# Ordering a whole encoder layer's instructions with another model of the machine

## The chip, the cores and the metric

The kernel runs on one core of a Trainium2 chip. The metric is the device time of one execution, in microseconds (us). The engines are TensorE (PE; its weight loads are listed as PEld), VectorE (DVE), ScalarE (ACT), GpSimd (POOL) and SyncE (SP, which here only issues DMAs).

## The reference

One encoder layer is applied to two sequences, `x_prompt` (1024 tokens) and `x_sample` (512 tokens), each of width 1024, in float32:

```
h  = x + token_mixer(rmsnorm(x))
h  = h + square(relu(rmsnorm(h) @ w_up)) @ w_down        # width 4096
y  = rmsnorm(h)

token_mixer(xn):
    z = xn @ w_in            # q_A k_A v_A q_B k_B v_B gate_A gate_B
    o_A = attention of 8 heads over all tokens, 2 key/value heads,
          q and k normalised and rotated
    o_B = attention of 8 heads over a clamped 8 x 16 window of the token grid,
          with a learned bias by relative position
    return (sigmoid(gate_A) * (o_A @ w_proj_a)
            + sigmoid(gate_B) * (o_B @ w_proj_b)) @ w_out
```

## The kernel before, in words

**Numbers.** Every float32 product is made of three matmuls: each operand is cut into a high part (an ACT copy into the matmul's format) and a low part (a DVE subtraction of that copy), and `mm3` (L194 to L197) adds high x high, high x low and low x high in PSUM. So each operand that TensorE takes has passed ACT and DVE before (`split`, L184 and L190; `cut`, L1273 and L1274).

**Stages.** The sequence of 512 tokens is worked through first, then that of 1024, each in this order (`run`): normalisation, and per group `g` of four heads the projections of branch A (`z`, `zv`), then the sweep of branch A (`s_tile`, L740 to L749: scores, row maximum, exponential, reciprocal, scaling on GpSimd; then transposes at L783, the cut into high and low at L788 and L789, and the product with V, `pv`, L759 and L760). Then branch B (`s_unit`, L971 to L982; `t_unit`, L994 to L1000; `v_unit`, L1013), its projections `qkproj` in between, and the merge (`ppa`, `ppb`, `op`). After both sequences comes the MLP over all 1536 tokens in two blocks of 768, with seven products of half-size blocks in place of eight (`up`, its products `ua` to `ud`; and the down projection, `dn`, whose stages run over 26 pairs of product and column group, six steps each). There the left operands are loaded as `ar` three pairs of steps ahead (`a_dma`) and cut two steps ahead (`a_step`).

**What sets the order.** The kernel's text is a trace: every instruction is written down once, in the order in which the Python code meets it. Matmuls that depend on nothing urgent, the gates (`gate`, tiles `gps`) and the first projection after attention (`proj_a`, tiles `ppa`), are generators in a list `fill`; the attention loops draw a few steps from it (`fill.pull`) between their own, so that TensorE has work while the softmax chain is on the other engines. When the context `tile.TileContext` closes, its scheduler plays the traced program on a model of the machine: on each engine it takes, of the instructions whose inputs are ready in the model, the one that was traced first. The order that comes out is compiled in; each engine then executes its own instructions in that order. Where `tc.keep_in_program_order` is called, the instruction is tied behind the one traced before it on its engine; this is done for most of the first operations of ACT, DVE and SP, and for the last ones of ACT and DVE. By default the model is the library's plain core simulator. Tiles come from pools with a fixed number of buffers (4 banks of PSUM in `pmm`, two double banks in `pbig`), so an instruction that opens a new tile is not ready until a buffer is free.

The whole layer is traced by `encoder(tc, ...)`, which `kernel` calls (L1795) inside the only context. The entry of that context is recorded under L1780, where the program object is made, and its exit (waits for all DMAs, drains, two synchronisations of all engines) under L1795.

Of the kernel before, what the change touches and what calls it, by code (L numbers as in the profile page):

```python
# [57 lines left out]
            self.pull(64)  # L58


@with_exitstack
def encoder(ctx: ExitStack, tc: tile.TileContext, xs, outs, w):
    nc = tc.nc
    dram = ctx.enter_context(tc.tile_pool(name="dram", bufs=1, space=bass.MemoryType.DRAM))
    cst = ctx.enter_context(tc.tile_pool(name="cst", bufs=1))
# [1733 lines left out]
```

## Time and profile before

| | |
|---|---|
| median of 3 runs | 2144.46 us (2144.26 to 2144.7) |
| the profiled execution's own time | 2144.47 us |
| its span, first to last instruction | 2142.7 us |
| mean granted TensorE clock | 0.999 |
| DMA moved | 354.08 MB, 165 GB/s over the span |

The profile tells, for each engine, when an instruction ran and what released it. Busy time is the union of an engine's instructions; matmuls overlap in the records, because the next one begins before the end of the one ahead is recorded. `x228` is a count, `L740` a line of the kernel, and `a<-b,c` what an instruction writes and reads, with buffer numbers left out. In rows by stretch, the first column is the stretch in us from the span's start, the second its length; then come busy times by engine, the granted clock, the busy share of the DMA engines and GB/s. In rows of groups, the numbers behind the bar are busy time in us, the mean of one in ns, and the idle time of the engine just before these instructions with what ended it.

### The profile page before, as it was taken

The page shows a single profiled execution, that of the slowest core. Times are in us where ns is not written, and L with a number is a line of the kernel's source. Part 1 is how long each engine was busy: PE and PEld are TensorE (multiplying, and loading weights), DVE is VectorE, ACT ScalarE, POOL GpSimd, SP SyncE. Part 2 cuts the span into 40 slices and gives each one's busy share as a digit, 9 for nine tenths or more (in the row PEclk, how much of TensorE's full clock was granted, in tenths as well). Part 3 has the DMA queues.
Part 4 walks back from the last instruction along what each step waited for, and adds up shares of the span by engine and source line. Part 5 has one row for each costly group of instructions (what it writes and reads, how often), then busy time and mean ns, then how long its engine had stood idle before and what let it go on. Part 6 is the DMA issues. An engine that isn't in the chain of part 4 may idle for free.

```text
span 2142.7 us, 32089 instructions
## 1 busy us (share of the span) xinstructions
PE 2115.4 (99%) x10967; PEld 1846.9 (86%) x10967; DVE 1462.8 (68%) x2793; ACT 1145.3 (53%) x2511; POOL 356.1 (17%) x446
## 2 busy tenths in 40 slices
PE   9999999999999999999999999999999999999998
PEld 8888778888897888887888899999999988888887
DVE  6665786767657755556882877778777777759563
ACT  6664653767566644555530566566555643434352
POOL 2232310323232223333200200003000000000000
PEclk9999999999999999999999999999999999999999
DMA  6437557520122133433472665578545799688561
GB/s 191 133 99 208 157 162 249 186 71 25 56 78 69 42 95 108 132 117 111 142 234 105 212 198 182 174 243 208 161 145 155 256 353 342 213 275 280 174 201 64
DMA packets 321259, 354.08 MB, mean 165 GB/s; under 512 B 31551, under 2 KB 255431, under 8 KB 321095
## 3 DMA queue, kind: packets, MB, share of 16 engines
q1 hardware_dynamic: 278647, 280.96, 42.0%
q10 hardware_dynamic: 35296, 50.88, 6.8%
q0 software_dynamic: 7152, 20.19, 3.5%
q8 instruction: 87, 1.43, 0.3%
q14 instruction: 77, 0.63, 0.1%
HBM read 264.85 MB, written 87.88 MB: 165 GB/s over the span
## 4 chain that ended last, share of the span: by engine, by line
PE 68%; issue 1%; DVE 1%; DMA 0%; ACT 0%; SPq 0%; POOL 0%; POOLq 0%; ACTq 0%; DVEq 0%
PE dn L196 7%; PE dn L197 7%; PE dn L195 7%; PE ua L195 2%; PE ua L197 2%; PE ua L196 2%; PE ud L195 2%; PE ud L197 2%; PE ud L196 2%; PE uc L195 2%; PE uc L197 2%; PE uc L196 2%; PE gpss L195 2%; PE gpss L197 2%; PE gpss L196 2%; PE ops L197 1%
## 5 line engine op out<-in xcount | busy, mean ns | idle before, releaser
L197 PE MATMUL dn<-wd,al 128*128 128x512 f32 x624 | 242.8, 389 | 0.0
L196 PE MATMUL dn<-wd,ah 128*128 128x512 f32 x624 | 242.8, 389 | 0.0
L195 PE MATMUL dn<-wd,ah 128*128 128x512 f32 x624 | 242.7, 389 | 0.0
L1273 ACT ACTIVATE ah<-ar 128x512 fp32r<-128x512 f32 x168 | 104.2, 627 | 202.6 <-PE dn L196 190.4
L1274 DVE TENSOR_TENSOR al<-ar,ah 128x512 fp32r<-128x512 f32 x168 | 114.0, 686 | 75.3 <-ACT ah L1273 67.2
L195 PEld LDWEIGHTS dn<-wd,ah 128*128 128x128 f32 x624 | 117.2, 188 | 24.5
L197 PEld LDWEIGHTS dn<-wd,al 128*128 128x128 f32 x624 | 117.2, 188 | 24.2
L196 PEld LDWEIGHTS dn<-wd,ah 128*128 128x128 f32 x624 | 117.2, 188 | 24.2
L749 POOL TENSOR_SCALAR ps<-ps,rls 128x1024 f32<-128x1024 f32 (+1 forms) x96 | 96.8, 1009 | 225.7 <-DVE rls L748 200.3
L788 ACT ACTIVATE pths<-pTs 128x512 fp32r<-128x512 f32 x160 | 94.0, 597 | 74.0 <-PE pTs L783 71.8
L789 DVE TENSOR_TENSOR ptls<-pTs,pths 128x512 fp32r<-128x512 f32 x160 | 107.5, 686 | 37.7 <-ACT pths L788 36.7
L743 DVE TENSOR_REDUCE nms<-ss 128x1 f32<-128x1024 f32 (+1 forms) x96 | 99.8, 1040 | 25.6 <-PE ss L741 25.1
L195 PE MATMUL gpss<-xs_0h,w_gs 128*128 128x512 f32 x256 | 105.6, 412 | 0.5 <-DVE ot_Bs L440 0.4
L746 ACT ACTIVATE ps<-ss,nms 128x1024 f32<-128x1024 f32 (+1 forms) x96 | 93.1, 971 | 22.8 <-DVE nms L743 20.1
L783 PEld LDWEIGHTS pTs<-ident,ps 128*128 128x128 f32 x640 | 78.0, 140 | 28.5 <-POOL ps L749 4.3
L180 POOL TENSOR_TENSOR rs_f<-ms_f,mhalf 128x1 f32<-128x1 f32 x6 | 4.0, 667 | 590.7 <-DVE ms_f L176 590.7
L197 PE MATMUL gpss<-xs_0h,w_gs 128*128 128x512 f32 x256 | 101.1, 395 | 0.3 <-DVE w_gs L190 0.3
L196 PE MATMUL gpss<-xs_0l,w_gs 128*128 128x512 f32 x256 | 101.0, 394 | 0.0
L783 PE MATMUL pTs<-ident,ps 128*128 128x128 f32 x640 | 99.0, 274 | 1.3 <-DVE ptls L789 0.6
L1273 ACT ACTIVATE A<-S 128x512 fp32r<-128x512 f32 x128 | 75.9, 623 | 31.2 <-DVE S L1336 22.4
L957 POOL TENSOR_TENSOR bms<-rects,msks 128x384 f32<-128x384 f32 (+1 forms) x72 | 70.1, 976 | 128.7 <-DVE nmbs L974 107.8
L1392 ACT ACTIVATE c<-c 128x384 f32<-128x384 f32 x96 | 50.3, 524 | 69.6 <-DVE c L1391 69.5
(330 smaller groups left out, 6418.7 us busy)
## 6 DMA issues: line engine op xcount, KB each, us to landing
ar<-ud SPq DMA_DIRECT2D x120, 512.0 KB, 5.2
br<-in_w_mlp_down_dram SPq DMA_DIRECT2D x72, 512.0 KB, 5.4
rawu<-in_w_mlp_up_dram SPq DMA_DIRECT2D x64, 512.0 KB, 4.1
ud<-c ACTq DMA_DIRECT2D x128, 192.0 KB, 3.3
raw_gs<-in_w_in_dram SPq DMA_DIRECT2D x32, 512.0 KB, 4.0
zgs<-sgs ACTq DMA_DIRECT2D x48, 256.0 KB, 2.2
ud<-cs SPq DMA_DIRECT2D x64, 192.0 KB
raw_os<-in_w_out_dram SPq DMA_DIRECT2D x16, 512.0 KB, 3.8
```

Source lines behind the costliest of these rows:

```text
L195: nc.tensor.matmul(out, ah, bh, start=start, stop=False, **kw)
L196: nc.tensor.matmul(out, ah, bl, start=False, stop=False, **kw)
L197: nc.tensor.matmul(out, al, bh, start=False, stop=stop, **kw)
L743: nc.vector.tensor_reduce(nm_, s, axis=AX.X, op=ALU.max, negate=True)
L746: nc.scalar.activation(p, s, AF.Exp, bias=nm_, accum_out=l)
L749: nc.gpsimd.tensor_scalar(p, p, rl, 1.0, op0=ALU.mult, op1=ALU.mult)
L783: nc.tensor.transpose(pt[:, j * P : (j + 1) * P], PP[u, j][:, kc * P : (kc + 1) * P], ident)
L788: nc.scalar.activation(hi, pt, AF.Copy)
L789: nc.vector.tensor_tensor(lo, pt, hi.bitcast(F32), op=ALU.subtract)
L957: nc.gpsimd.tensor_tensor(bm.rearrange("p (r c) -> p r c", c=32), rects[h][:, ir : ir + kr_n, jr : jr + 32], msk[:, hf * 3 + ct, :].rearra ...
L1273: nc.scalar.activation(hi, src, AF.Copy)
L1274: nc.vector.tensor_tensor(lo, src, hi.bitcast(F32), op=ALU.subtract)
```

## The change

`encoder` becomes a wrapper; the function that was `encoder` is called `layers` and is not edited. The wrapper opens a critical section of the outer context, and in it a second context on the same program object, with `schedule_with_timeline_sim=True`. That flag makes the scheduler play the program on the library's timeline simulator, a different model of the machine, in place of the plain core simulator. The outer context, which now holds nothing but this section, is still opened and closed by `kernel`. All pins, pools, buffer counts, queues and the text's order stay as they are.

```diff
+def encoder(outer, xs, outs, w):
+    with outer.tile_critical(), tile.TileContext(outer.nc, schedule_with_timeline_sim=True) as tc:
+        layers(tc, xs, outs, w)
+
+
 @with_exitstack
-def encoder(ctx: ExitStack, tc: tile.TileContext, xs, outs, w):
+def layers(ctx: ExitStack, tc: tile.TileContext, xs, outs, w):
     nc = tc.nc
```

## The prediction

> **What bounds the kernel now.** I read the head of the page first, then the busy time of each engine by stage, then the waits of TensorE alone, and last the groups of instructions from which the terms below are made.
>
> ```profile
> span 2142.7 us, 32089 instructions
> ...
> PE 2115.4 (99%) x10967; PEld 1846.9 (86%) x10967; DVE 1462.8 (68%) x2793; ACT 1145.3 (53%) x2511; POOL 356.1 (17%) x446
> ```
>
> TensorE is busy for 2115.4 of 2142.7 us. An order of the instructions changes neither their number nor their work, so all that a new order can win from waiting is 2142.7 - 2115.4 = 27.3 us, 1.3% of the span. The next view says where these 27.3 us lie. Its columns are the stretch, its length, and the busy time of PE, PEld, DVE, ACT and POOL in it.
>
> ```profile
> 0.00:50.00 50.00, 45.10 (x296) 41.80 (x297) 32.44 (x70) 33.62 (x110) 13.45 (x23) 1.00 0.63 184
> 50.00:450.00 400.00, 390.94 (x2085) 330.63 (x2084) 276.18 (x671) 236.55 (x644) 104.56 (x149) 1.00 0.54 167
> 450.00:755.00 305.00, 302.62 (x1700) 256.65 (x1699) 208.81 (x361) 196.78 (x455) 90.09 (x86) 1.00 0.18 55
> 755.00:1030.00 275.00, 273.42 (x1334) 224.95 (x1333) 162.80 (x435) 142.73 (x293) 91.16 (x113) 1.00 0.41 116
> 1030.00:1205.00 175.00, 175.00 (x815) 144.78 (x814) 110.93 (x206) 60.41 (x108) 23.96 (x32) 1.00 0.52 173
> 1205.00:1710.00 505.00, 503.44 (x2873) 496.45 (x2872) 383.00 (x647) 306.83 (x607) 25.61 (x31) 1.00 0.61 190
> 1710.00:2135.00 425.00, 424.94 (x1876) 351.69 (x1874) 286.42 (x407) 166.36 (x292) 6.74 (x11) 1.00 0.73 240
> ```
>
> Subtract the second number from the first in each row. The first 50 us lose 4.9. The two token mixers (50 to 1205 us: projections, the two attentions, gates, merge) lose 9.06 + 2.38 + 1.58 + 0.00 = 13.0. The MLP, from 1205 to 2135 us, loses 1.56 + 0.06 = 1.6, and the last 7.7 us of the span hold no matmul. So an order can win at most 1.6 us in the MLP, nearly half of the program, and what there is to win lies in the mixers and the head.
>
> ```profile
> PE ss L740 <- ACT kTs L594: 2.5, 3, 1.2
> ```
>
> This is the largest entry among TensorE's own waits: 2.5 us in three waits, the longest 1.2. The loss is thus made of many waits of about a microsecond or less at changes from one kind of work to another, and not of one stage with a bottleneck.
>
> **The change, part by part.** It puts the whole program into a second context inside the first and lets another model of the machine choose the order. It removes no instruction of the computation and no DMA. There are three terms.
>
> First, the second context. It has an entry and an exit of its own. The exit of the context is recorded under line 1795, the entry under 1780:
>
> ```profile
> L1795 SPq EVENT_SEMAPHORE  x11: 17/28/28, 2138.5 to 2142.6; - x11
> ...
> L1795 SPq DRAIN  x3: 7/7/7, 2141.4 to 2142.1; - x3
> ```
> ```profile
> L1780 PEldq EVENT_SEMAPHORE  x1: 51/51/51, 0.7 to 0.7; - x1
> ```
>
> From the first SyncE drain at 2141.4 us to the end of the span are 1.3 us; from its first wait at 2138.5 they are 4.2, but the front of that is the flight of the last output. The entry is over at 0.7 us. A second exit and entry therefore cost between 1.3 and 4.2 + 0.7 = 4.9 us; they only add instructions on a path that nothing hides, so there is no gain on this side. I take 1.3 + 0.7 = 2.0, because a second exit finds the outputs already landed.
>
> Second, what a better fitting order can take back: some part of the 13.0 us of the mixers. The head's first operations are pinned on ACT, DVE and SP by hand, and the pins stay, so I give the 4.9 us there nothing. The rows cannot tell which of the waits have a ready matmul that could be put ahead; the term lies between 0 and -13.0. I take the middle, -6.5.
>
> Third, what a new order can newly expose. In the attention stages TensorE's time is filled by gate matmuls (`gps`), which the program text hands out a few at a time between the steps of softmax. An order made by readiness takes a gate matmul whenever the traced one is not ready by the model, so it tends to spend this filler earlier than the text does. What is then uncovered is the chain from a score tile to the operands of its product with V. Branch A first, then branch B; columns at the end are the count, the busy time and the mean ns of one.
>
> ```profile
> L743 DVE TENSOR_REDUCE nms<-ss 128x1 f32<-128x1024 f32 (+1 forms) x96 | 99.8, 1040 | 25.6 <-PE ss L741 25.1
> L746 ACT ACTIVATE ps<-ss,nms 128x1024 f32<-128x1024 f32 (+1 forms) x96 | 93.1, 971 | 22.8 <-DVE nms L743 20.1 <-DVE rls L748 2.3
> L748 DVE RECIPROCAL rls<-ls 128x1 f32<-128x1 f32 x96 | 15.1, 158 | 18.9 <-ACT ps L746 18.0
> L749 POOL TENSOR_SCALAR ps<-ps,rls 128x1024 f32<-128x1024 f32 (+1 forms) x96 | 96.8, 1009 | 225.7 <-DVE rls L748 200.3 <-DMA zgs<-sgs 11.8 <-PE pTs L783 11.7
> L783 PE MATMUL pTs<-ident,ps 128*128 128x128 f32 x640 | 99.0, 274 | 1.3 <-DVE ptls L789 0.6 <-POOL ps L749 0.3
> L788 ACT ACTIVATE pths<-pTs 128x512 fp32r<-128x512 f32 x160 | 94.0, 597 | 74.0 <-PE pTs L783 71.8
> L789 DVE TENSOR_TENSOR ptls<-pTs,pths 128x512 fp32r<-128x512 f32 x160 | 107.5, 686 | 37.7 <-ACT pths L788 36.7
> ```
> ```profile
> L974 DVE CUSTOM_DVE_ANT_0 sbss<-sbs,bms 128x384 f32<-128x384 f32 (+1 forms) x96 | 48.6, 507 | 43.8 <-PE sbs L971 37.0 <-issue 3.7 <-POOL pbs L982 1.8
> L979 ACT ACTIVATE pbs<-sbss,nmbs 128x384 f32<-128x384 f32 (+1 forms) x96 | 55.4, 577 | 36.5 <-DVE nmbs L974 32.1 <-DVE rlbs L981 1.6 <-POOL bms L957 1.0
> L981 DVE RECIPROCAL rlbs<-lbs 128x1 f32<-128x1 f32 x96 | 14.7, 153 | 12.2 <-ACT pbs L979 11.9
> L982 POOL TENSOR_SCALAR pbs<-pbs,rlbs 128x384 f32<-128x384 f32 (+1 forms) x96 | 58.9, 616 | 77.7 <-DVE rlbs L981 52.2 <-PE ptbs L994 9.2 <-PE ppas L197 6.7
> L994 PE MATMUL ptbs<-ident,pbs 128*128 128x128 f32 x256 | 39.1, 273 | 0.7 <-ACT sgs L429 0.4 <-DVE rlbs L981 0.2
> L999 ACT ACTIVATE bhs<-ptbs 128x384 fp32r<-128x384 f32 (+1 forms) x96 | 40.7, 453 | 12.2 <-PE ptbs L994 10.1 <-ACT pbs L979 0.8
> L1000 DVE TENSOR_TENSOR bhs<-ptbs,bhs 128x384 fp32r<-128x384 f32 (+1 forms) x96 | 46.2, 504 | 9.1 <-ACT bhs L999 8.1
> ```
>
> Branch A: 1040 + 971 + 158 + 1009 + 274 + 597 + 686 = 4735 ns, 4.7 us. Branch B: 507 + 577 + 153 + 616 + 273 + 453 + 504 = 3083 ns, 3.1 us. There are four sweeps of A (two groups in each of two sequences) and two stages of B. If the filler runs out before a stage does, one such chain stands open at its end; the next stage's projections, ready by then, can cover part of it. With half of each chain covered this is 4 x 2.35 + 2 x 1.55 = 12.5 us. The lower end is 0 (the filler lasts). For the upper end I ask what a stage costs if its gates are all spent in its first half. These are the stages, and then the gate matmuls in them (and the `ppa` ones, which fill the end of the first B stage); the third column is PE:
>
> ```profile
> 150.00:310.00 160.00, 156.32 (x777) 126.89 (x775) 114.24 (x336) 94.75 (x219) 45.65 (x68) 1.00 0.60 172
> 450.00:560.00 110.00, 108.06 (x574) 87.44 (x573) 82.15 (x132) 72.95 (x131) 33.57 (x29) 1.00 0.15 44
> 650.00:755.00 105.00, 104.91 (x563) 85.62 (x562) 78.16 (x124) 71.92 (x127) 34.31 (x30) 1.00 0.15 45
> ```
> ```profile
> 150.00:310.00 160.00, 64.86 (x228) 39.38 (x228) 5.97 (x10) 1.00 0.60 172
> 450.00:560.00 110.00, 42.76 (x146) 25.58 (x144) 3.60 (x6) 1.00 0.15 44
> 650.00:755.00 105.00, 38.98 (x132) 23.06 (x130) 3.00 (x5) 1.00 0.15 45
> 755.00:1030.00 275.00, 110.31 (x417) 75.72 (x417) 10.78 (x18) 1.00 0.41 116
> ```
> ```profile
> 150.00:310.00 160.00, 25.68 (x96) 16.73 (x96) 5.42 (x8) 1.00 0.60 172
> ```
> ```profile
> 2131.31 0.23 PE dn L197
> ```
>
> Matmuls overlap in the records, so I count them at the 0.23 us step that the last chain of the program shows for a 128x512 one. The sweep at 450 us then has 108.06 - 146 x 0.23 = 74.5 us of other TensorE work; its half, 37.2, stands against half of DVE's 82.15, 41.1: 3.9 us lost. At 650 us: (104.91 - 30.4) / 2 = 37.3 against 39.1, 1.8 lost. At 150 us, without gates and `ppa`: (156.32 - 52.4 - 22.1) / 2 = 40.9 against 57.1, 16.2 lost. At 755 us TensorE stays the longer (88.8 against 81.4) and nothing is lost. Together 22, which comes on top of open ends in the worst case.
>
> The sum, against the profiled execution's own 2144.47 us (span 2142.7, 1.8 around it; the median of the runs shown is 2144.46, so the two are one number): 2144.47 + 2.0 - 6.5 + 12.5 = 2152.5. Its ends: 2144.47 + 1.3 - 13.0 = 2132.8 below, 2144.47 + 4.9 + 12.5 + 22 = 2183.9 above.
>
> The MLP I cost at nothing: its stages lose 1.6 us in 930, so nearly every matmul is ready in the order of the text, and a pick by readiness and then by that order leaves it. What covers it are the loads' leads; rival three prices their loss.
>
> One rule speaks for more room than I allow. The Trainium skill ("Perfetto Trace Analysis", section Identifying the Most-Contended Engine) says that matmul busy time is not a good measure of how near TensorE is to its limit, and that the busy share of the weight loads is one of the two that are. By it the 86% would leave 14%, an estimate of 300 us, to a better order. The trace differs: from 1710 to 2135 us the weight loads are busy for 351.69 of 425, 83%, while the matmuls there wait for nothing (424.94 of 425) and follow at their even 0.23 us. A share of 83 to 86% is full pace here.
>
> **The rivals.** One, the other side: the new model foresees readiness better, filler lasts, and order only takes waits away. For it: the waits are short and scattered, as from a model that is a little wrong everywhere. Three quarters of the 13.0 go, no end opens: 2144.5 + 2.0 - 9.8 = 2136.7. A second gain lies beside this: changing between kinds of work costs time in the records,
>
> ```profile
> L195 PE MATMUL gpss<-xs_0h,w_gs 128*128 128x512 f32 x256 | 105.6, 412 | 0.5 <-DVE ot_Bs L440 0.4
> ```
> ```profile
> L197 PE MATMUL dn<-wd,al 128*128 128x512 f32 x624 | 242.8, 389 | 0.0
> ```
>
> 412 against 389 ns for the same shape, 256 x 23 ns = 5.9 us in this group; an order in longer runs of one kind would save some of it. With 9.8 us taken back this rival decides while less than 3.5 us of the 12.5 come (2.0 - 9.8 + 3.5 = -4.3, the bound of what can be told). The skill's 14% is its extreme: weight loads packed into the idle 14%, 2144 - 300 = 1844; against it stands the 83% row, and I give it 1 in 100.
>
> Two: the order hardly differs where it matters, gains and losses cancel, only the second context is left: 2144.5 + 2.0 = 2146.5. That the timeline model reproduces today's order, so the change does not do what it says, gives the same number. For it: TensorE is never far from ready work in any stage.
>
> Three, slower by much: SP's loads in the down projection are reordered.
>
> ```profile
> ar<-ud SPq DMA_DIRECT2D x120, 512.0 KB, 5.2
> ```
>
> A pair of steps (24 matmuls of 0.23 us, 5.5 us) is loaded three pairs, 16.5 us, ahead; the tile is needed 5.2 us plus the split (about 1.3 us as L788 and L789) after issue, 6.5 in all. It decides when the lead falls below 6.5, by two pairs; each pair then waits 6.5 - 5.5 = 1.0 us, and 78 pairs make 78: 2144.5 + 2.0 + 78 = 2224. Against it: two pairs of slack, and no wait on such a load in TensorE's 424.94 of 425 us.
>
> **How the numbers follow.** About 0.2%, 4.3 us, is what can be told from no change. Slower as forecast, 2152.5: 39 in 100, its own range 2149 to 2184. Rival one, faster: 30, and the skill's extreme 1. Rival two, no change: 25. Rival three: 5. So faster 0.31, same 0.25, slower 0.44; that the sign is little more than a guess lies in the second and third terms, both of which are bounded but not seen. The range goes from the lower end of the sum, 2132, to its upper, 2184; outside stay the extreme, rival three and the tails of the others, some 12 in 100.
>
> **What would show it.** Right: two sets of exit instructions and an end about 1 to 2 us later after the last output; gate matmuls earlier within each attention stage, and then windows near 160, 310, 580, 770 and 1030 us with PE busy some 2 us less than their length and waits on DVE or ACT of the softmax chain; the MLP stretch unchanged at 930 us. Wrong: PE idle in 50 to 1205 us below 10 us (rival one); idle of 13 us in the same places as now (rival two); TensorE waits on `ah` or `al` after 1710 us (rival three).

## The result: 127 us slower, a tenth of it from the context and the rest from the order

The changed kernel takes 2271.4 us (median of 3 runs, 2267.6 to 2278.0) against 2144.5: 1.0596 times as long, interval 1.0557 to 1.0635. The prediction said slower, by 8 us; it is 127. One execution of the experiments stands apart and is left out of its ratio: one of the four of the order alone took 3522 us, at a granted clock of 0.56. The profile is of the changed kernel's 2278.0 us execution. Its head, its clock by slices and the chain that ended last:

```profile
span 2276.2 us, 32090 instructions
...
PE 2159.3 (95%) x10967; PEld 1881.1 (83%) x10967; DVE 1454.9 (64%) x2793; ACT 1147.9 (50%) x2511; POOL 348.4 (15%) x446
...
PEclk9999999999999999999999999999999889999999
...
PE 80%; DMA 6%; DVE 5%; issue 4%; ACT 3%; SPq 1%; POOL 1%; ACTq 0%; POOLq 0%; DVEq 0%
```

The same matmuls are there (x10967), and TensorE's busy time grew by 44 us although no work was added; its idle time grew from 27 to 117. The granted clock falls in two slices near 1800 us. By stage (the columns are those of the prediction's table):

```profile
0.00:50.00 50.00, 39.82 (x250) 37.05 (x251) 24.51 (x53) 25.12 (x87) 11.82 (x21) 0.97 0.71 210
50.00:450.00 400.00, 359.20 (x1713) 293.76 (x1712) 236.85 (x589) 200.03 (x480) 79.15 (x124) 0.94 0.48 145
450.00:750.00 300.00, 289.50 (x1696) 254.59 (x1695) 189.34 (x364) 186.33 (x548) 88.51 (x94) 0.99 0.24 71
750.00:1100.00 350.00, 342.71 (x1705) 284.06 (x1705) 213.60 (x510) 187.98 (x375) 105.97 (x130) 1.00 0.33 96
1100.00:1290.00 190.00, 185.21 (x867) 154.50 (x865) 118.22 (x225) 66.03 (x121) 28.76 (x39) 1.00 0.52 171
1290.00:1790.00 500.00, 497.67 (x2837) 491.05 (x2836) 379.62 (x636) 310.49 (x598) 26.10 (x29) 1.00 0.60 186
1790.00:1870.00 80.00, 55.34 (x215) 45.49 (x216) 34.03 (x51) 24.68 (x44) 0.00 (x0) 0.79 0.83 292
2040.00:2085.00 45.00, 38.10 (x144) 30.07 (x145) 36.06 (x51) 12.10 (x22) 0.00 (x0) 0.89 0.75 244
```

Two places stand out: the first sequence's mixer (50 to 450 us: 40.8 us idle, at 0.94 of the clock), and the first 80 us of the down projection, 24.7 idle at 0.79. The up projection (1290 to 1790) is as full as before. TensorE's own waits:

```profile
PE dn L200 <- ACT ah L1278: 24.2, 3, 16.1
PE ss L745 <- ACT ps L751: 14.4, 14, 4.3
PE dn L202 <- DVE al L1279: 7.2, 4, 2.9
PE ua L200 <- ACT B L344: 4.8, 1, 4.8
```

Before, the longest of all such waits was 1.4 us. Now one lasts 16.1 us, and the score matmuls `ss` wait for the exponentials `ps`: there are two buffers for score tiles (`pbig`), and one is free only when the exponential has read it.

Below, *loss* means loss against full pace: over all pairs of matmuls in a row, the time from start to start less the pace that most matmuls of its shape show (226 ns for 512 columns, 173 for 384, 118 for 256, 92 for 128), summed. It holds idle time and slow matmuls alike. "Mixers" is here all that lies ahead of the MLP's first matmul, the first 50 us included. Before: 73.5 us in the mixers, 4.4 in the MLP. Changed: 157.1 and 52.6.

### The profile page after: what moved, and what is told of

Same layout as the page of the kernel before. It is cut to its first block, busy times and chain, and to the rows that moved or that the text cites. A ratio compares the mean times of both kernels' runs of the same rounds, so it can differ in the third digit from the quotient of the medians.

```text
span 2276.2 us, 32090 instructions
## 1 busy us (share of the span) xinstructions
PE 2159.3 (95%) x10967; PEld 1881.1 (83%) x10967; DVE 1454.9 (64%) x2793; ACT 1147.9 (50%) x2511; POOL 348.4 (15%) x446
## 4 chain that ended last, share of the span: by engine, by line
PE 80%; DMA 6%; DVE 5%; issue 4%; ACT 3%; SPq 1%; POOL 1%; ACTq 0%; POOLq 0%; DVEq 0%
PE dn L200 6%; PE dn L202 6%; PE dn L201 6%; PE gpss L200 3%; PE gpss L201 3%; PE gpss L202 3%; PE pTs L788 2%; PE ua L200 2%; PE ua L201 2%; PE ua L202 2%; PE uc L202 2%; PE uc L201 2%; PE uc L200 2%; PE ud L200 2%; PE ud L202 2%
## 5 line engine op out<-in xcount | busy, mean ns | idle before, releaser
L200 PE MATMUL dn<-wd,ah 128*128 128x512 f32 x624 | 248.0, 398 | 24.2 <-ACT ah L1278 24.2
L201 PE MATMUL dn<-wd,ah 128*128 128x512 f32 x624 | 247.0, 396 | 0.0
L200 PEld LDWEIGHTS dn<-wd,ah 128*128 128x128 f32 x624 | 119.9, 192 | 50.5 <-ACT ah L1278 25.4
L201 PEld LDWEIGHTS dn<-wd,ah 128*128 128x128 f32 x624 | 120.0, 192 | 25.2
L1278 ACT ACTIVATE wd<-br 128x512 fp32r<-128x512 f32 x96 | 58.0, 624 | 82.3 <-PE dn L202 24.8
L1279 DVE TENSOR_TENSOR A<-S,A 128x512 fp32r<-128x512 f32 x128 | 85.7, 687 | 21.5 <-ACT A L1278 21.4
```

The costliest lines, as they stand in the source:

```text
L200: nc.tensor.matmul(out, ah, bh, start=start, stop=False, **kw)
L201: nc.tensor.matmul(out, ah, bl, start=False, stop=False, **kw)
L1278: nc.scalar.activation(hi, src, AF.Copy)
L1279: nc.vector.tensor_tensor(lo, src, hi.bitcast(F32), op=ALU.subtract)
```

## The experiments

Beside all of them the kernel before had medians of 2143.9 to 2145.1 us. The second context alone and the new order alone come first, as the two can be had apart: without the flag, the inner context gives every queue exactly the order of the kernel before, and with the flag on the one outer context every queue has exactly the order of the changed kernel.

**The context without the order.**

```diff
-    with outer.tile_critical(), tile.TileContext(outer.nc, schedule_with_timeline_sim=True) as tc:
+    with outer.tile_critical(), tile.TileContext(outer.nc) as tc:
```

> The second context stays, the timeline flag goes; every queue then stands as in the kernel before, instruction by instruction. Theory O (the new order alone costs the time): the context costs its entry and exit only, about 0.2 + 1.4 us by the two traces, so 2146 us. Theory C (the nested context itself costs: the DMA issues of SP, whose median went from 384 to 599 ns in the changed kernel, and the waits that follow from them): half or more of the 127 us stays, 2205 us or more, and SP's issues have a median near 599 ns here too.

Measured: 2157.1 us, 1.0057 (1.0042 to 1.0072): 12.6 us more than before. Neither theory has the size: the context costs far more than its entry and exit, and far less than half of the 127 us.

**The order without the context.**

```diff
-    with tile.TileContext(nc) as tc:
+    with tile.TileContext(nc, schedule_with_timeline_sim=True) as tc:
```

> The flag is set on the one outer context and the second context goes; every queue stands as in the changed kernel, instruction by instruction. Theory O: 2271 less 1.6 us of entry and exit, so 2266 to 2272 us, with the 16 us stall of TensorE at the start of the down projection and SP's issues at either 384 or 599 ns. Theory C: 2210 us or less, SP's issues back at 384 ns.

Measured: 2248.1 us, 1.0479 (1.0461 to 1.0496): 103.6 us. With the 12.6 that makes 116.2 of 126.9; 11 us come only when both are there. The time lies between what the theories name (O 2266 or more, C 2210 or less), but the order is the main cause. The issues of the operand loads `ar` (duration in ns: min/median/max), in before, changed, context alone and order alone, one fence each:

```profile
L1452 SPq DMA_DIRECT2D ar<-ud x120: 359/363/3407, 1409.9 to 2084.5; - x120
```
```profile
L1457 SPq DMA_DIRECT2D ar<-ud x120: 579/581/998, 1493.4 to 2219.7; - x120
```
```profile
L1457 SPq DMA_DIRECT2D ar<-ud x120: 579/587/3213, 1418.2 to 2093.3; - x120
```
```profile
L1452 SPq DMA_DIRECT2D ar<-ud x120: 359/360/1613, 1474.1 to 2190.2; - x120
```

The long issues go with the context, not with the order.

**The long issues without the context.** The compiled program of the kernel before carries a mark on most DMA starts of SP and ScalarE that those of the inner context lack. Taking it off in the kernel before:

```diff
     nc = _bacc.Bacc("TRN2", target_bir_lowering=False, num_devices=1)
+    nc.dge_precook = False
```

> The kernel before, one context, every queue in the same order; only the mark goes that the compiled program carries on 908 of SP's 916 and 206 of ScalarE's 278 DMA starts, and that no DMA start of the nested context carries. Theory I (the context's 12.6 us are its longer DMA issues): SP's issues have a median of 600 ns and ScalarE's of 458 as in the context alone, and the time is 2144.5 + 12.6 - 1.6 (entry and exit) = 2155.5 us. Theory X (the context costs by something else, its blocks or its semaphores): the issues lengthen or not, the time stays at 2144 to 2147 us.

Measured: 2153.6 us, 1.0042 (1.0027 to 1.0057), and the issues of `ar` at a median of 587 ns. Theory I holds: 9.0 of the context's 12.6 us are longer DMA issues. The 3.6 left are near the prediction's 2.0 for entry and exit, and the executions of the context alone spread by 5.6 us.

**Half of the program held.** A helper ties each instruction of a queue behind the one that stands ahead of it in the kernel before (an edge of issue order that waits for nothing). In the cuts of the code here and below, names stand for the packed lists of the orders:

```diff
+    for a, b in zip(seq, seq[1:]):
+        tc.add_manual_dep(
+            b, a.name, mybir.DependencyInfo(mybir.DependencyClass.NoSync, mybir.DependencyReason.DATA), reason="hold"
+        )
...
+    for engine in ("PE", "SP", "Activation", "DVE", "Pool"):
+        hold(tc, engine, order_before[engine], "mix")
```

The other run has "mlp" in place of "mix".

> The changed kernel, but the five queues are held to their order in the kernel before for all that the mixers trace; only the MLP's part is ordered by the timeline model. Theory O with costs that add up stage by stage: the MLP's loss against full pace was 49 us in the changed kernel and 3 us before, so 2144.5 + 1.6 + 46 = 2192 us, with the stall of some 16 us at the start of the down projection. Theory M (the MLP's stalls are the echo of a disturbed SP queue and late stores in the mixers): without the cause they go, 2146 to 2155 us.

> The other half: the MLP's queues are held to their order in the kernel before, the mixers are ordered by the timeline model. Theory O with costs that add up: 2144.5 + 1.6 + 79 (loss of the mixers 152 us in the changed kernel against 73 before) = 2225 us. Theory M: the MLP's stalls come with the mixers' disorder, so 2255 us or more.

Measured: mixers held 2200.5 us, 1.0260 (1.0243 to 1.0278); MLP held 2225.6, 1.0379 (1.0363 to 1.0394). Over the 2157.1 of the context alone that is 43.4 us for the MLP's order and 68.5 for the mixers', together 111.9 of 114.3: the two add up, and theory M falls; theory O's sums were 2192 and 2225. With the mixers in their old order the down projection stalls just as long, TensorE's waits there:

```profile
PE dn L219 <- ACT ah L1297: 24.6, 3, 17.4
PE dn L221 <- DVE al L1298: 7.1, 4, 2.9
```

**One queue held, or some, over the whole program.** The same helper, by engine; the others are ordered by the timeline model around what is held. "Producers" are ScalarE, VectorE and GpSimd.

> The changed kernel, with TensorE's queue held to its order in the kernel before; the other four queues are ordered by the timeline model around it. Theory P (the mixers lose by TensorE's own order, the gates spent in clumps ahead of the score chains; the MLP by the load order): 2157 (context) + 43 (the MLP ordered by the model: 2200.5 - 2157) + a few us = 2200 to 2210 us, with the stalls near 70, 157, 257 and 305 us gone. Theory V (the mixers lose because the vector and scalar producers stand in another order): they stay, 2240 us or more.

> The changed kernel, with SP's queue alone held to its order in the kernel before. Theory S (the MLP's loss is SP's load order at the start of the down projection): the stall of 16 us near 1801 to 1817 us and the two of 4 us behind it go with the half-speed stretches there: 2271 - 35 = 2236 us, the mixers' stalls unchanged. Theory A (ScalarE's own queue, where the stores wait between the cuts, holds the operands back): 2262 us or more, the stall still there.

> The changed kernel, with the queues of ScalarE, VectorE and GpSimd held to their order in the kernel before; TensorE and SP are ordered by the timeline model. Theory P: TensorE's clumps of gates are still there, and so is SP's load order: 2255 us or more. Theory V: the mixers' stalls go, 2271 - 68 = 2203 us or less.

> The changed kernel with the queues of TensorE and SP both held to their order in the kernel before; ScalarE, VectorE and GpSimd are ordered by the timeline model. Theory D (the costs of the queues add up): 2271.4 - 37.6 (TensorE held) - 41.4 (SP held) = 2192 us, so 35 us over the 2157 us of the context alone, and those are the producers' order by itself. Theory Q (the producers' order hurts only through the matmul and load order that goes with it): 2157 to 2165 us.

> The changed kernel with TensorE, ScalarE, VectorE and GpSimd held to their order in the kernel before; SP alone is ordered by the timeline model. Theory S (the load order costs what holding it took back): 2157 + 41 = 2198 us, with a stall of 9 to 17 us at the start of the down projection. Theory E (the loads come late there only because the up projection's stores and cuts had moved too): 2170 us or less.

> The changed kernel with SP, ScalarE, VectorE and GpSimd held to their order in the kernel before; TensorE alone is ordered by the timeline model. This is the prediction's third step by itself. Theory F (as predicted, the gates spent early leave four half chains open): 2157 + 13 to 35 us, 2170 to 2192 us. Theory K (orders of two queues that were not made together clash: TensorE takes the work that the model's producers would have ready): 2333 (SP free) - 41 = 2292 us.

| held to the order of before | us | ratio, interval | over the context alone | loss, mixers / MLP |
|---|---|---|---|---|
| all (context alone) | 2157.1 | 1.0057 (1.0042 to 1.0072) | 0 | 81.3 / 4.4 |
| TensorE, producers | 2186.2 | 1.0194 (1.0179 to 1.0209) | 29 | 90.2 / 30.9 |
| TensorE, SP | 2189.0 | 1.0210 (1.0194 to 1.0225) | 32 | 103.6 / 16.9 |
| SP | 2230.0 | 1.0399 (1.0384 to 1.0415) | 73 | 145.5 / 16.1 |
| TensorE | 2233.8 | 1.0416 (1.0401 to 1.0432) | 77 | 117.7 / 48.7 |
| none (the change) | 2271.4 | 1.0596 (1.0557 to 1.0635) | 114 | 157.1 / 52.6 |
| SP, producers | 2307.2 | 1.0762 (1.0745 to 1.0778) | 150 | 215.7 / 24.4 |
| producers | 2333.0 | 1.0877 (1.0859 to 1.0895) | 176 | 219.1 / 49.0 |

Holding TensorE gives 37.6 us back, nearly all in the mixers; holding SP 41.4, three quarters of it in the MLP (its loss falls by 36.5 us, the mixers' by 11.6, where theory S had the mixers unchanged); holding both 82.4, so these two add up (theory D, within 3.3 us), and 32 us remain for the producers' order. For TensorE alone held neither theory hits: 2233.8 lies between P's 2210 and V's 2240. Some stalls go (the 4.1 us at 307 us), others come (4.6 us at 241 us, a wait for the head's cut `kBs`). With SP alone in the new order (second row) 2186.2 lies between theory S's 2198 and E's 2170, but the stall that S names is there with all other queues as before:

```profile
PE dn L219 <- ACT ah L1297: 17.3, 2, 12.6
```

So the stall at the start of the down projection needs no queue but SP's to change. In the last two rows the producers are in the old order and TensorE in the new one, and the kernel is *slower* than with both new: 2307.2 is near theory K's 2292 and far from F's 2170 to 2192, and 2333.0 rules out theory V's 2203 or less. A reading that no run tests by itself: TensorE asks for operands in an order in which nobody makes them.

**Sixteen loads pinned.** In the down projection, SP's starts of the block loads `hs` and of the kept down weights `tb`, before and then changed:

```profile
L1624 SPq DMA_DIRECT2D hs<-hd x8: 408/500/727, 1700.4 to 1834.6; - x8
...
L1473 SPq DMA_DIRECT2D tb<-in_w_mlp_down_dram x8: 460/466/1063, 1758.7 to 1809.3; - x8
```
```profile
L1629 SPq DMA_DIRECT2D hs<-hd x8: 580/856/1855, 1784.5 to 1799.8; - x8
...
L1478 SPq DMA_DIRECT2D tb<-in_w_mlp_down_dram x8: 601/1055/2676, 1801.7 to 1818.7; - x8
```

What was spread over 134 us (1700 to 1835) now starts within 34 us, and each start takes about twice as long. Among them on SP's queue stand the operand loads `ar`:

```profile
L1457 SPq DMA_DIRECT2D ar<-ud x2: 580/584/588, 1786.2 to 1821.9; - x2
```

That row is of 1786 to 1823 us: two starts, 35.7 us apart. A pair of steps needs one or two every 5.5 us and is loaded 16.5 us ahead. In the long stall the DMA engines were full (the last two columns are their busy share and GB/s):

```profile
1803.00:1807.00 4.00, 0.00 (x0) 0.00 (x0) 0.32 (x1) 0.98 (x2) 0.00 (x0) 0.57 1.05 386
```

Before, their share was 0.97 to 1.06 from 1700 to 1820 us and no matmul waited, so full DMA engines alone do not stall TensorE: it matters what they move first. The sixteen loads move 10.5 MB (eight of 768 KB, eight of 512 KB), an estimated 27 us at the 386 GB/s of that row. Whether the operand loads were late by their place in SP's queue or by these bytes ahead of them, the next run does not separate.

```diff
-                    nc.sync.dma_start(tt2(g * 4 + 2 * i), wd_v[1, g, :, 2 * i : 2 * i + 2, 512:1024])
+                    op = nc.sync.dma_start(tt2(g * 4 + 2 * i), wd_v[1, g, :, 2 * i : 2 * i + 2, 512:1024])
+                    tc.keep_in_program_order(op)
...
-                nc.sync.dma_start(
+                op = nc.sync.dma_start(
                     hs[q][:, :, hc], hd[q * 3 * P : (q + 1) * 3 * P, hc].rearrange("(t p) c -> p t c", p=P)
                 )
+                tc.keep_in_program_order(op)
```

> The changed kernel, with the loads of hs and of tb (the blocks and the down weights that the down projection keeps, 16 DMA starts) pinned behind the DMA that is traced ahead of each on SP's queue; all else is ordered by the timeline model. Theory B (the 12 of them that stand in a row ahead of the operand loads make the stall of 16 us): that stall goes, 2271.4 - 30 to 40 = 2231 to 2241 us. Theory W (the other weight loads and the stores hold the operand loads back as well): 2255 us or more, a stall of 8 us or more still there.

Measured: 2237.3 us, 1.0433 (1.0418 to 1.0449), 34.1 back; theory B. The stretch that had 55.34 of 80 us at 0.79 of the clock:

```profile
1790.00:1870.00 80.00, 79.88 (x356) 66.59 (x355) 58.04 (x79) 34.09 (x61) 0.00 (x0) 0.99 0.98 329
```

**The gates placed.** This is the prediction's third step by itself. In the changed kernel the gate matmuls do go early and in clumps. These are the gates alone (second number in brackets: how many) in the 11.3 us ahead of a sweep's first scores and in the 15.7 us of its start, where the program text would spread them:

```profile
142.10:153.40 11.30, 11.28 (x48) 1.00 0.59 180
153.40:169.10 15.70, 5.98 (x19) 0.78 0.53 148
```

```diff
     for a, b in zip(seq, seq[1:]):
+        if picked is not None and b.name not in picked:
+            continue
...
+    hold(tc, "PE", order_before["PE"], "all", only=gates)
```

> The changed kernel, with one thing held in TensorE's queue: each of the 1152 gate matmuls (those that write gps) stands behind the instruction that is ahead of it in the kernel before; all else is ordered by the timeline model. Theory G (the mixers' loss by TensorE's order is the gates spent early): most of the 37.6 us that holding the whole queue gave back, 2234 to 2245 us, and the stall of 4.4 us at 159 us gone. Theory R (it is the rest of the queue: projections and head transposes ahead of the score chains): 2258 us or more.

Measured: 2267.4 us, 1.0576 (1.0558 to 1.0593): 4.0 us back, theory R. The gates in runs of more than 12 fell from 783 of 1152 to 135 (87 before), so the clumps are gone, and the mixers' loss only went from 157.1 to 148.8. The waits of the scores for `ps` fell from 14.4 to 6.8 us, but the sweep's stall is still there (3.7 us at 155 us), and TensorE now waits elsewhere too: at the transposes for `ptls` 8.6 us in place of 0.8, once 3.5 us for `kTs` at 61 us and once 5.8 for `kBs` at 249.

> Both edits at once. If G and B hold and add up: 2271.4 less the two gains, 2195 to 2210 us, and what stays over the 2157 us of the context alone is the producers' order (32 us by the run with TensorE and SP held) and a few us more. If the gates are held and the loads are not to blame, or the other way round: 2225 to 2240 us.

Measured: 2233.3 us, 1.0413 (1.0398 to 1.0429): 38.0 = 34.1 + 4.0. They add up; what stays is 76 us over the context, not the 38 to 53 of the expectation, which reckoned with 26 us or more from the gates.

**The cuts placed.** The chain of waits that leads to the stall at 159 us (start, length, what; lines between are left out) names another step:

```profile
151.74 4.37 DMA raw_gs<-in_w_in_dram
...
156.13 0.02 ACT w_gs L189
...
157.21 0.60 ACT sgs L434
...
158.42 0.07 ACT ps L751
...
159.25 0.80 PE ss L745
```

ScalarE stands at `w_gs`, the cut of a gate's weights into high and low part, until their load lands at 156.1; the exponentials that the scores need are behind it in the same queue. Over the mixers, ScalarE's idle time that a DMA's landing ended (pieces over 0.3 us) went from 33 to 96 us.

```diff
+    hold(tc, "Activation", order_before["Activation"], "all", only=cuts)
+    hold(tc, "DVE", order_before["DVE"], "all", only=cuts)
```

> The changed kernel, with one thing held: each cut of a loaded weight into its high and low part (134 on ScalarE, 268 on VectorE) stands behind the instruction that is ahead of it on its engine in the kernel before; all else is ordered by the timeline model. Theory T (a cut whose load has not landed stands at the head of ScalarE's queue and holds the score chain behind it): ScalarE's waits for DMA in the mixers fall from 96 us to 40 or 55, the stall at 159 us goes, and the time falls by 30 to 60 us, to 2211 to 2241 us. Theory U (part of a queue in one order and part in another clash, as when all producers were held, 2333 us): 2271 us or more.

> Cuts, gates and loads held as in the three runs with one of them. Theory T with gains that add up: 2233 (gates and loads) less 30 to 60, 2173 to 2203 us; what then stays over the 2157 us of the context alone is all else that the model moves. Theory U: 2233 us or more.

Measured: cuts 2252.7 us, 1.0504 (1.0488 to 1.0520), 18.7 back; all three 2207.3, 1.0288 (1.0271 to 1.0305), 64.1 back, of which the cuts are 26 on top of the other two. The mechanism is there (ScalarE's waits for DMA in the mixers fall from 96 to 67 us), but for less than the 30 to 60 us expected; neither theory has the 2252.7. The stall at 159 us is gone, but in the same run a gate matmul waits 7.6 us for its own cut, `w_gs`. The edit moves the cuts on ScalarE and VectorE together, so ScalarE's share is not separated. 50 us over the context stay.

**SP's whole queue with cuts and gates.** Ahead of that gate's load, sixteen loads of `vss` stand in a row on SP, changed and then before:

```profile
L883 SPq DMA_DIRECT2D vss<-vds x16: 555/595/1778, 139.2 to 151.0; - x16
```
```profile
L878 SPq DMA_DIRECT2D vss<-vds x16: 302/425/431, 124.1 to 147.5; - x16
```

The edit holds all of SP in place of the sixteen loads of the MLP.

> The changed kernel, with SP's whole queue held to its order in the kernel before, and the cuts of loaded weights and the gate matmuls placed as in the runs before. Theory Y (bursts of loads on SP delay operands in the mixers as they do in the MLP): 10 to 25 us less than with the MLP's loads alone, 2182 to 2197 us, and the mixers' loss falls from 120 to 110 us or less. Theory Z (what stays in the mixers is the order of the vector work itself): 2200 us or more, the mixers' loss at 118 us or more.

Measured: 2201.5 us, 1.0263 (1.0245 to 1.0280), the mixers' loss 117.3: 5.9 us less than with the MLP's loads alone. Theory Z in time, its mark for the loss missed by 0.7: of what the mixers still lose, the order of loads is little.

**Stalls by themselves.** In the kernel before, the down projection goes at full pace, so a stall's price can be read there.

```diff
+            for _ in range(more):
+                nc.scalar.activation(hi, r[0][:, :, (j % 2) * P : (j % 2 + 1) * P], AF.Copy)
             cut(hi, lo, r[0][:, :, (j % 2) * P : (j % 2 + 1) * P])
```

> The kernel before with eight stalls put into the down projection, where TensorE otherwise goes at full pace: at eight places, 18 operands apart, ScalarE writes the same high part again 8, 10, 12, 14, 16, 18, 22 and 28 times before VectorE reads it; nothing else is computed. Theory H (a long stall costs its length and then a stretch at half the granted clock; the ten runs so far show such a stretch after every stall over 3.8 us, after some between 2.0 and 3.8 us and after few below): stalls of about 1 to 9 us, half-speed stretches of 3.4 us or more behind the longer ones, and the time up by the sum of the stalls plus half of what the stretches hold outside the stalls. Theory N (the half-speed stretches are marks of the idle time and take no time of their own): the time up by the sum of the stalls alone.

Measured: 2159.4 us, 1.0071 (1.0054 to 1.0088). Only two of the eight stopped TensorE for long, those of 18 and of 28 writes; that of 22 cost it 0.6 us. The smaller of the two (start, length in us of single matmuls):

```profile
1992.89 0.39 PE L197 MATMUL dn<-wd,al 128*128 128x512 f32 x1
1996.06 0.78 PE L195 MATMUL dn<-wd,ah 128*128 128x512 f32 x1 [2.78 <-ACT ah L1275]
1996.64 0.63 PE L196 MATMUL dn<-wd,ah 128*128 128x512 f32 x1
1997.07 0.63 PE L197 MATMUL dn<-wd,al 128*128 128x512 f32 x1
1997.49 0.63 PE L195 MATMUL dn<-wd,ah 128*128 128x512 f32 x1
```

From 1996.64 on the matmuls follow at 0.43 us in place of 0.23, until 1999.6; the granted clock is half for 3.4 us. The stall is 2.94 us and the loss 4.70; the other is 6.41 and 9.23 with 6.8 us at half clock. The two stalls are 9.4 us and the span grew by 14.6 (2157.2 - 2142.7, unrounded): theory H.

## Why the prediction was wrong

**The step that failed is "The MLP I cost at nothing".** Its reason was that nearly every matmul is ready in the order of the text, and that a pick by readiness then leaves that order. That is true of TensorE: held or not, the up projection keeps its pace. But the pick is made on SP's queue too, and there the sixteen loads of `hs` and `tb` were taken ahead of the operand loads. The MLP's order costs 43.4 us, of which 34.1 are sixteen loads. The sentence that followed named the cover ("the loads' leads") and rival three priced its loss, but at 78 us spread over 78 pairs and with 5 chances in 100, from the slack on average. What came was one burst that left the operand loads out for 35.7 us once. The evidence against it, that no such wait showed in 424.94 of 425 us, spoke of the old order.

**The third term was mis-sized, and its cause was another.** Forecast 12.5 us (0 to 34.5) for gates spent early; the mixers' order costs 68.5. The gates do go early, as forecast, and windows near 160 and 310 us show the stalls, now of 4 us. But placing the gates gives 4.0 us back: where filler is put back, the scores' waits for `ps` halve and TensorE waits for `ptls`, `kTs` and `kBs` in their place. What is shown of the 68.5 are 19 to 26 us for the place of the weight cuts; the one stall that was followed back led to a cut that waited for its load at the head of ScalarE's queue. Holding all of TensorE and SP leaves 32 us to the producers' order; which of their instructions, beyond the cuts, and which of TensorE's, beyond the gates, stays open. The upper bound of 34.5 let one chain stand open per stage and moved TensorE's queue alone, where the new order moves all five.

**The second term, -6.5 us taken back, does not show.** No version with any part of the new order came out faster than the context alone.

**The first term was right in place and short in size.** There are two sets of exit instructions, of the inner and the outer context:

```profile
L62 SPq DRAIN  x4: 7/7/7, 2273.7 to 2274.8; - x4
```
```profile
L1800 SPq DRAIN  x3: 7/7/7, 2275.1 to 2275.4; - x3
```

From the first drain to the end are 2.5 us, against 1.3 before. But the second context was taken to add instructions only. It also made every marked DMA start longer, which no row of before could show: 9.0 us.

**A term was missing: the clock.** The prediction's first view took TensorE's busy time as fixed and only its 27.3 us of idle time as open to a new order; busy time grew by 44 us with the same matmuls. The changed kernel's trace has sixteen stretches at half of the granted clock, 105.8 us together, and before has none until after its last matmul. Counting only matmuls at about twice their pace in them, 26 of the 132 us of added loss are this. The Trainium skill ("TensorE: Matmul & The Clock Gate", section HAM oscillation — how this bites in real kernels) has the rule that TensorE should not idle for more than about 3.4 us, or it goes on cold. The traces agree and go further: of all single stalls in the twenty traces, 52 of 52 of 3.8 us or more have such a stretch beside them (from 1 us before to 7 us behind), 67 of 86 between 2.0 and 3.8 us, 32 of 100 between 1.5 and 2.0 (not counted: in seventeen of the traces one of 2.4 to 2.7 us in the first 6 us, ahead of the trace's first record of the clock). At the measured 4.70 us for a stall of 2.94 and 9.23 for 6.41, a stall of that size costs about one and a half times its length, and the prediction priced its open chains at their bare length.

**What held:** the sign, in part by luck: the prediction itself called it little more than a guess, and of the terms behind it the gates gave 4.0 us where 12.5 were forecast, while most of the 127 us came by what it had at nothing or did not name; the rule on weight loads weighed against the trace (no room of 300 us appeared, and 83% of weight loading is now the share of a kernel that stalls); the end of the program. Of the signs named for rival three, waits on `ah` and `al` after 1710 us came true to the letter.

The sum after the fact: 12.6 for the context (9.0 of it DMA issues), 43.4 for the MLP's order, 68.5 for the mixers', 2.4 left over: 126.9.

## What to carry to other kernels

A stage in which the bottleneck engine never waits is not safe from a new order: ask of each queue what is ready early and could be put ahead of the load that the stage lives on, and look at the spacing of those loads' starts. Orders of several queues belong together; hold them one at a time and in pairs before naming one as the cause, since half an order can be worse than the whole. When a wrapper is added, compare the duration of the DMA starts, not only the entry and exit.

## What the hardware showed that I had not expected

- A DMA start without the compiled mark occupies SP for 581 to 587 ns at the median in place of 363 (`ar`), and ScalarE for 458 in place of 327 (all its starts); GpSimd's stay at 580.
- Stretches at half clock come in steps of about 3.4 us (70 of 148 are of 3.4, 63 of 6.8, the longest 20.5), and a stall of 2.9 us is enough for one: it cost 4.7 us.
- While the sixteen loads of `hs` and `tb` were issued in a row, a single start took up to 2.7 us on SP (`tb`: median 1.06, shortest 0.60; before 0.47 at the median), so the queue that issued the burst slowed too: pinned, the starts of `tb` have a median of 0.61. Single long starts are found outside a burst as well (`ar`, up to 3.4 us before).
